# Five instead of four pairs of token chunks through the seven-product form of an output projection

## The chip, the core and the metric

The kernel runs on one core of one Trainium2 chip. The metric is the device time of one execution in microseconds (us); lower is better. The engines are named as the profile names them: PE (TensorE, matmul), PEld (its weight load), DVE (VectorE), ACT (ScalarE), POOL (GpSimd) and SP (SyncE). SP issues almost all transfers here, and its queue is worked off in order: a transfer that must wait holds everything behind it.

## What is computed

One encoder layer over 2048 tokens of width 1024. A combined input projection feeds a gated linear attention (four heads) and a latent attention (four heads, swept in query blocks). Their outputs are joined to a row of width 1024, multiplied by one 1024x1024 matrix, added to the scaled input, and normalised:

```python
return jnp.concatenate([o_a, o_b], axis=-1) @ w_out
...
x = layer_norm(DEEPNORM_ALPHA * x + mixed, ln_g[layer], ln_b[layer])
```

Only the last two steps, the output projection with its residual and LayerNorm, are touched by the change.

## The kernel before

The tokens are cut into 16 chunks of 128. Every matmul in full precision is done as three matmuls on a high and a low part of each operand (`mm3`: high by high, high by low, low by high), so each left operand is first split: ACT copies it to the rounded high part (`hi`), POOL subtracts to get the low part (`lo`).

The output projection starts while the last attention block is still running and then fills the rest of the program. For chunk c, `load` fetches the attention outputs `oa` (group A) and `ob` (group B) into a tile `of`, and two factors (`gm`, the gate, and `r`, the softmax's reciprocal) into `gr`; `gate` multiplies `ob` by both on POOL; `load_res` fetches the input rows `xr`. A plain chunk is 8 steps of the inner dimension k by two halves n of 512 columns, three matmuls each: 48 matmuls of 128x512 into two PSUM banks. `residual` then adds the scaled input on DVE and takes statistics, `finish_a` and `finish_b` normalise (two DVE instructions each per chunk), and two stores of 256 KB go out. `banks` says which PSUM banks a chunk uses: `pS` (two tiles of two banks) or the single banks `mb`, `x`, `o`, `ap`.

Chunks 8 to 15 go in four pairs through `Pair`. A pair is a 2x2 block product: two row blocks (the two chunks) by two halves of the inner dimension, against a 2x2 cut of the matrix. It is done in seven products of half the inner dimension instead of eight (P1 to P7, 12 matmuls each, 84 for a pair where two plain chunks have 96). For that, sums of the left blocks are formed on DVE (`add`: S1 to S4), seven operands are split instead of four per two chunks, and the products are added up on DVE (`sum`, `read`) with two copies by ACT (`copy`). The sums of weight blocks lie in DRAM as `wt1` to `wt4` and are fetched by `fetch_t`; `wt4` replaces, in place, the second column half of the first four rows of the matrix, which plain chunks need, so it is fetched after the last plain chunk has used them. In a pair P1 writes bank `mb` (`pw0`), P5 bank `x` (`pw1`), P6 bank `o` (`pw2`) and P3 bank `ap` (`pw3`).

Two more pieces of work belong to this stretch. The last attention block (number 15) is closed late: `tot`, `oh`, `ol` prepare its sum and split its output, `tsum` and `turn` are transposes, `y` a product of three matmuls into bank `o`, and `yc` and `rows` are ACT copies that are stored. And `ln_psum` copies the LayerNorm scale and shift from SBUF into a PSUM tile, after which their SBUF tiles `lng` and `lnb` serve odd pairs as `of` tiles.

The order of instructions is given by hand: `PLACE_PAIR` holds, for each step of a pair, its time relative to the pair's start, `PAIR_US` the distance of two pairs, and `put` collects steps that are then sorted by place. Inside `fixed()` ACT, POOL and SP keep the order in which the code is written. `PAIR0` is the first chunk of the first pair.

Of the kernel before, what the change touches and what calls it, by code (L numbers as in the profile page):

```python
# [9 lines left out]
F32 = mybir.dt.float32  # L10
# [8 lines left out]
P = 128  # L19
# [3 lines left out]
NCH = S // P  # L23
# [4 lines left out]
QB = 512  # L28
# [102 lines left out]
)  # L131


PAIR0, PAIR_US = 8, 19.05
PLACE_PAIR = dict(
    load3=(-29.4, -31.5),
    load2=(-25.5, -31.5),
# [252 lines left out]
class K:  # L390
# [1224 lines left out]
    def attention(self):  # L1615
# [4 lines left out]
        with ExitStack() as ctx:  # L1620
# [147 lines left out]
            def tsum(i):  # L1768
                d = stt[i]
                d["x"] = close(i, [P, 4, P], f"sx{i}", (pA, "ap"))  # L1770
                for e in range(4 if i == nb - 1 else 2):
                    nc.tensor.transpose(d["x"][:, e], d["as"][:, 0, e * P:(e + 1) * P], self.ident)

            def rcp(i):

                d = stt[i]
                rc = op.sm.tile([P, 4], F32, tag="rc", name=f"rc{i}")
                if i == nb - 1:
                    V.tensor_reduce(rc, d["x"], AX.X, ALU.add)
                else:  # L1780
                    V.tensor_reduce(rc.rearrange("p (e j) -> p j e", e=2),
                                    d["x"][:, 0:2].rearrange("p j (e k) -> p j e k", e=2), AX.X, ALU.add)
                V.reciprocal(rc, rc)
                d["rc"] = rc
# [56 lines left out]
            def put(place, fn, *a):  # L1841
                todo.append((place, len(todo), fn, a))
# [62 lines left out]
            rest = {c: o for c, o in enumerate(first)}  # L1905

            def load(c):
                if c < NCH:
                    rest[c] = dict(c=c)
                    op.load(rest[c])  # L1910

            def split(c):
                if c < NCH:
# [4 lines left out]
                    op.gate(rest[c])  # L1918
                    op.hi(rest[c], 1)
                    op.lo(rest[c], 1)  # L1920

# [2 lines left out]
            with fixed():  # L1924
                load(4)
                for c in (2, 3):
                    op.load_res(rest[c])
                load(5)
                split(4)
                load(6)  # L1930
# [8 lines left out]
                for c in (2, 3):  # L1939
                    op.residual(rest[c], 0)  # L1940
                    op.residual(rest[c], 1)
                    op.finish(rest[c])
            for c in (4, 5):
                with fixed():
                    if c == 4:
                        split(6)
                        pairs[0].load(1)
                        op.product(rest[4])
                    else:
                        op.load_res(rest[6])  # L1950
                        tsum(nb - 1)
                        with self.after(rest[4]["last"]):
                            rcp(nb - 1)
                        op.product(rest[5])
                        op.ln_psum(0)
                        pairs[1].load(0, "of")
                        op.fetch_t("3m")
                        split(7)
                        pairs[0].load(0)
                    op.finish(rest[c])  # L1960
                if c == 4:
                    with self.after(*last.values()), fixed():
                        for f in (tot, oh, ol):
                            f(nb - 1)

            todo.clear()
            half = 5.44
            put(4 * half - 0.01, op.pair_banks)
            for c in (6, 7):
                o, t = rest[c], 2 * half * (c - 6)  # L1970
                if c == 7:
                    put(-1, op.load_res, o)
                for n in range(2):
                    for k in range(NK):
                        put(t + half * n, op.part, o, k, (n,))
                    put(t + half * (2 if c % 2 else n + 1) + 0.05, op.residual, o, n)
                put(t + 2 * half + 1.3, op.finish_a, o)
                put(t + 2 * half + (5 if c == 6 else 4), op.finish_b, o)
            for place, f in ((5.4, turn), (5.41, y), (6.5, rows), (6.51, yc)):
# [10 lines left out]
class Pair:  # L1990
# [131 lines left out]
    def put(self, put, T, last):  # L2122
# [2 lines left out]
        first = P_[("first", "second")[self.p]] if self.p < 2 else {}  # L2125
        if self.p:
            for r in (1, 0):
                at(P_[f"load{self.p}"][r], self.load, r, *(("gr",),) * (self.p == 1 and r == 0))
        for r in range(2):
            at(P_["res"][r], self.load_res, r)  # L2130
# [54 lines left out]
class OutProj:  # L2185
# [140 lines left out]
    def residual(self, o, n):  # L2326
        nc, c = self.nc, o["c"]
        if n == 0:
            o["rr"] = self.bp.tile([P, 2, 512], F32, tag="ph", name=f"rr{c}", bufs=3)
            o["bn"] = self.sm.tile([P, 2, 6], F32, tag="bn", name=f"bn{c}")  # L2330
        rr = o["rr"][:, n]
        nc.vector.scalar_tensor_tensor(rr, o["xr"][:, n], ALPHA, o["ps"][n], ALU.mult, ALU.add)
        o["last"] = nc.vector.bn_stats(o["bn"][:, n], rr).ins
# [103 lines left out]
```

## Time and profile before

| what | us |
|---|---|
| time, median of 3 runs | 1276.11 (1275.75 to 1276.61) |
| the profiled execution's own time | 1276.71 |
| its span in the trace | 1274.9 |
| first plain matmul of chunk 4 | 1145.86 |
| first product of the first pair | 1190.67 |
| last matmul starts | 1266.86 |

Times inside the trace count from the span's start. A row of the timeline gives start, duration, engine, line, operation, output and input tiles, how many instructions were merged (x2), and in brackets how long the engine sat idle just before and what ended it.

### The profile page before, as it was taken

The numbers are of one execution on the slowest core, as the hardware profiler recorded it, in microseconds if no ns is written. First come the engines' busy times: TensorE is split into PE (matmuls) and PEld (weight loads), VectorE is DVE, ScalarE is ACT, GpSimd is POOL, SyncE is SP. The second block draws the span as 40 slices with busy tenths as digits, with TensorE's granted clock in tenths as the row PEclk, the third lists the DMA queues.
The fourth block names the chain that finished last, engine by engine and source line by source line (L and its number), as shares of the span: only waits on it lengthen the run. The fifth ranks groups of instructions, "written<-read, shape, count | busy, mean of one in ns | idle before, by whom it ended". The sixth has DMA issues, their size and how long they took to land.

```text
span 1274.9 us, 20185 instructions
## 1 busy us (share of the span) xinstructions
PE 1254.0 (98%) x6928; PEld 1109.7 (87%) x6928; DVE 939.2 (74%) x1704; ACT 873.7 (69%) x1537; POOL 849.5 (67%) x550
## 2 busy tenths in 40 slices
PE   7999999999999999999999999999999999999997
PEld 7999999999999999999788888888888888788886
DVE  6866675656675455555798888888888889738887
ACT  7765656766676656665588888888888888624355
POOL 0144545363667666672188888889999999965774
PEclk9999999999999999999999999999999999999999
DMA  9332524343675565555501111122223111568962
GB/s 300 98 94 63 170 79 159 102 156 102 196 249 172 179 220 183 182 198 170 170 1 42 42 43 42 42 58 59 59 58 91 52 43 31 173 207 295 355 200 100
DMA packets 122662, 166.81 MB, mean 131 GB/s; under 512 B 18518, under 2 KB 71390, under 8 KB 121920
## 3 DMA queue, kind: packets, MB, share of 16 engines
q1 hardware_dynamic: 114400, 163.39, 40.1%
q0 software_dynamic: 768, 2.10, 0.5%
q8 instruction: 55, 0.90, 0.3%
q10 hardware_dynamic: 7392, 0.03, 0.3%
q14 instruction: 47, 0.39, 0.1%
HBM read 106.72 MB, written 58.75 MB: 130 GB/s over the span
## 4 chain that ended last, share of the span: by engine, by line
PE 65%; ACT 2%; DVE 1%; POOL 1%; issue 1%; DMA 0%; DVEq 0%; ACTq 0%
PE pS L1649 4%; PE o L456 4%; PE o L454 4%; PE o L455 4%; PE pS L1650 4%; PE pS L1651 4%; PE pS L1652 4%; PE pS L1653 4%; PE pz L455 2%; PE pz L456 2%; PE pz L454 2%; PE pw L455 2%; PE pw L454 2%; PE pw L456 2%; PE ipm L456 1%; PE ipm L454 1%
## 5 line engine op out<-in xcount | busy, mean ns | idle before, releaser
L406 POOL TENSOR_TENSOR pl<-s,ph 128x1024 fp32r<-128x1024 f32 x128 | 306.1, 2415 | 56.5 <-ACT ph L400 56.5
L1671 DVE TENSOR_TENSOR rm<-pS,rm 128x512 f32<-128x512 f32 x210 | 144.7, 689 | 26.4 <-ACT s L1658 20.8
L1695 DVE TENSOR_TENSOR s<-s,mb 128x1024 f32<-128x1024 f32 x128 | 151.2, 1213 | 9.4 <-PE mb L1689 9.3
L1658 ACT ACTIVATE s<-pS 128x1024 f32<-128x1024 f32 x128 | 131.4, 1026 | 37.7 <-PE pS L1653 33.5
L400 ACT ACTIVATE ph<-s 128x1024 fp32r<-128x1024 f32 x128 | 135.0, 1057 | 13.4 <-PE o L456 12.7
L1699 ACT ACTIVATE s<-s 128x1024 f32<-128x1024 f32 x128 | 131.5, 1051 | 13.4 <-DVE s L1695 13.3
L454 PE MATMUL ipa<-wah,xah 128*128 128x384 f32 (+1 forms) x384 | 130.2, 339 | 6.7 <-ACT wah L400 6.7
L1112 POOL TENSOR_TENSOR Us<-Us,cw 128x512 f32<-128x512 f32 x16 | 18.2, 1135 | 175.4 <-DVE Us L1110 167.4
L456 PE MATMUL ipa<-wah,xal 128*128 128x384 f32 (+1 forms) x384 | 125.3, 326 | 0.0
L455 PE MATMUL ipa<-wal,xah 128*128 128x384 f32 (+1 forms) x384 | 125.0, 325 | 0.0
L1649 PE MATMUL pS<-qh,ckvT_h 128*128 128x512 f32 x256 | 102.6, 401 | 0.8 <-DVE rm L1671 0.4
L454 PE MATMUL o<-ph,vh 128*128 128x512 f32 x256 | 101.1, 395 | 0.0
L1650 PE MATMUL pS<-ql,ckvT_h 128*128 128x512 f32 x256 | 99.9, 390 | 0.0
L1651 PE MATMUL pS<-qh,ckvT_l 128*128 128x512 f32 x256 | 99.9, 390 | 0.0
L1652 PE MATMUL pS<-rh,krs 128*128 128x512 f32 x256 | 99.8, 390 | 0.0
L1653 PE MATMUL pS<-rl,krs 128*128 128x512 f32 x256 | 99.8, 390 | 0.0
L456 PE MATMUL o<-ph,vl 128*128 128x512 f32 x256 | 99.8, 390 | 0.0
L455 PE MATMUL o<-pl,vh 128*128 128x512 f32 x256 | 99.7, 389 | 0.0
L1722 DVE TENSOR_TENSOR ap<-ap,s 128x512 f32<-128x512 f32 x120 | 83.0, 692 | 3.5 <-ACT s L1699 0.9
L454 PEld LDWEIGHTS ipa<-wah,xah 128*128 128x128 f32 x384 | 73.4, 191 | 7.3 <-ACT wah L400 6.7
L454 PE MATMUL pz<-xch,wzh 128*128 128x256 f32 x256 | 74.8, 292 | 0.0
L455 PEld LDWEIGHTS ipa<-wal,xah 128*128 128x128 f32 x384 | 73.5, 191 | 0.8 <-DVE wal L406 0.2
(447 smaller groups left out, 3895.4 us busy)
## 6 DMA issues: line engine op xcount, KB each, us to landing
xcf<-xT_dram SPq DMA_DIRECT2D x16, 512.0 KB, 5.0
xr<-x_dram SPq DMA_DIRECT2D x16, 512.0 KB, 6.4
xaf<-xT_dram SPq DMA_DIRECT2D x14, 512.0 KB, 3.8
wb<-wO_dram SPq DMA_DIRECT2D x16, 256.0 KB, 3.0
oib<-oi_s SPq DMA_DIRECT2D x16, 256.0 KB, 4.3
qdb<-qd_s SPq DMA_DIRECT2D x16, 256.0 KB, 4.5
SU<-su_s SPq DMA_DIRECT2D x16, 256.0 KB, 4.7
ub<-u_s SPq DMA_DIRECT2D x16, 256.0 KB, 4.3
```

The costliest lines, as they stand in the source:

```text
L400: return nc.scalar.activation(dst, src, AF.Copy).ins
L406: return e.tensor_tensor(dst, src, hi.bitcast(F32), ALU.subtract).ins
L454: mm(out, ah, bh, start=start, stop=False)
L455: mm(out, ah, bl, start=False, stop=False)
L456: mm(out, al, bh, start=False, stop=stop)
L1649: mm(ps[:, e], kh, qh, start=True, stop=False)
L1650: mm(ps[:, e], kh, ql, start=False, stop=False)
L1651: mm(ps[:, e], kl, qh, start=False, stop=False)
L1652: mm(ps[:, e], kr, rh, start=False, stop=False)
L1653: mm(ps[:, e], kr, rl, start=False, stop=True)
L1671: V.tensor_tensor(d["rm"], src[:, e], d["rm"], ALU.max)
L1695: V.tensor_tensor(s, s, d["mb"][:, None, :].to_broadcast([P, 2, QB]), ALU.subtract)
```

## The change

`PAIR0` goes from 8 to 6: chunks 6 and 7 become a pair, and only chunks 0 to 5 are plain. Everything else adapts the surroundings. Chunks 4 and 5 both use the single banks `mb` and `x` (before, chunk 5 had a `pS` tile). Chunk 5 adds its residual in the tile of its input rows. `yc` gets the buffer `ofh` in place of `ofl`, which the first pair's copies use. The written order of the stretch ahead of the pairs changes: loads, splits, `finish` calls and the closing of block 15 are interleaved differently, and in `PLACE_PAIR` the first pair's residual loads and one gate move. The first pair now loads where the plain chunk 6 did.

```diff
-PAIR0, PAIR_US = 8, 19.05
+PAIR0, PAIR_US = 6, 19.05
...
-    gate0=((-6.0, -4.7), (-24.72, -21.3)),
+    gate0=((-11.0, -10.9), (-24.72, -21.3)),
...
-    first=dict(hA11=-15.2, hS3=-8.0, hA12=0.9, lS3=-6.5, aS4=0.3, hS4=0.35, lS4=0.4),
+    first=dict(res=(-18.7, -18.6), hA11=-15.2, hS3=-8.0, hA12=0.9, lS3=-6.5, aS4=0.3, hS4=0.35, lS4=0.4),
...
-                t = bp.tile([P, QB], F32, tag="ofl", name=f"yc{i}", bufs=1)
+                t = bp.tile([P, QB], F32, tag="ofh" if i == nb - 1 else "ofl", name=f"yc{i}", bufs=1)
...
+                op.finish(rest[0])
+                split(4, 0)
+                op.finish(rest[1])
+                split(4, 1)
+                op.residual(rest[2], 0)
+                op.residual(rest[2], 1)
+                pairs[0].load(1)
                 op.load_res(rest[4])
-                for c in (0, 1):
-                    op.finish(rest[c])
-                split(5)
-                load(7)
+                with self.after(*last.values()):
+                    for f in (tot, oh, ol):
+                        f(nb - 1)
+                split(5, 0)
+                op.finish(rest[2])
+                split(5, 1)
+                pairs[0].load(0)
                 op.load_res(rest[5])
                 op.fetch_t("2l")
                 op.fetch_t("3h")
...
-            for c in (6, 7):
-                o, t = rest[c], 2 * half * (c - 6)
-                if c == 7:
-                    put(-1, op.load_res, o)
+            for c in (4, 5):
+                o, t = rest[c], 2 * half * (c - 4)
...
-            put(17.15, op.fetch_t, "4h")
-            put(17.16, op.fetch_t, "4l")
+            put(1.5, op.ln_psum, 0)
+            put(5.6, op.finish_a, rest[3])
+            put(10.96, op.finish_b, rest[3])
+            put(6.4, pairs[1].load, 0, "of")
+            put(11.9, op.fetch_t, "3m")
+            put(17.05, op.fetch_t, "4h")
+            put(17.06, op.fetch_t, "4l")
...
-        if c == PAIR0 - 1:
-            return [p.tile([P, 512], F32, tag=t, name=f"p{t}{c}") for p, t in self.single[2:]]
-        if c < 2 or c % 2:
+        if c < 2 or c == PAIR0 - 3:
             ps = self.ps.tile([P, 2, 512], F32, tag="pS", name=f"po{c}")
...
-            o["rr"] = self.bp.tile([P, 2, 512], F32, tag="ph", name=f"rr{c}", bufs=3)
+            o["rr"] = o["xr"] if c == PAIR0 - 1 else self.bp.tile([P, 2, 512], F32, tag="ph", name=f"rr{c}", bufs=3)
```

The first place is DVE where chunk 1 is finished and chunk 2's two banks (`pmb2`, `px2`) are read, which chunk 4's matmuls write next. `rr` is a chunk's result tile, the number behind a name its chunk. Before:

```order
L1743 COPY acc15_12969<-ap15_12370 128x512
L2345 BN_AGGR mv1_12785<-bn1_12678 128x2
L2346 TENSOR_SCALAR u1_12786<-mv1_12785 128x1
L2348 SCALAR_TENSOR_TENSOR rr1_12677<-rr1_12677,mv1_12785,lng_12573 128x512 x2
L2332 SCALAR_TENSOR_TENSOR rr2_12826<-xr2_12738,pmb2_12557 128x512
```

The same place on DVE now, from the second half of chunk 1's residual on:

```order
L2352 SCALAR_TENSOR_TENSOR rr0_12647<-rr0_12647,ln0_r_12758,lnb_12574 128x512
L2318 BN_STATS bn1_12678<-rr1_12677 128x6
L1743 COPY acc15_12811<-ap15_12370 128x512
L2330 BN_AGGR mv1_12774<-bn1_12678 128x2
L2331 TENSOR_SCALAR u1_12775<-mv1_12774 128x1
L2333 SCALAR_TENSOR_TENSOR rr1_12677<-rr1_12677,mv1_12774,lng_12573 128x512 x2
L2352 SCALAR_TENSOR_TENSOR rr1_12677<-rr1_12677,ln1_r_12784,lnb_12574 128x512 x2
L2317 SCALAR_TENSOR_TENSOR rr2_12798<-xr2_12738,pmb2_12557 128x512
```

The two closing instructions of chunk 0 and the two of chunk 1 now stand ahead of the read of `pmb2`; before, all four stood behind it.

The second place is SP behind chunk 5's loads. Before:

```order
L2277 DMA of5_12742<-ob_s1_165 128x4x128
L2274 DMA of6_12758<-oa_s6_150 128x512
L2275 DMA gr4_12733<-gm_s1_141 128x4x128
L2276 DMA gr4_12733<-r_s1_161 128x4x128
L2277 DMA of6_12758<-ob_s1_165 128x4x128
L2296 DMA xr4_12763<-x_dram 128x1024
L2368 DMA out_dram<-rr0_12647 128x512 x2
L2368 DMA out_dram<-rr1_12677 128x512 x2
```

And now:

```order
L2264 DMA of5_12742<-ob_s1_165 128x4x128
L2353 DMA out_dram<-rr0_12647 128x512 x2
L2353 DMA out_dram<-rr1_12677 128x512 x2
L2000 DMA of6_12804<-oa_s6_150 128x512
L2003 DMA gr4_12733<-gm_s1_141 128x4x128
L2004 DMA gr4_12733<-r_s1_161 128x4x128
L2006 DMA of6_12804<-ob_s1_165 128x4x128
L2283 DMA xr4_12809<-x_dram 128x1024
L2353 DMA out_dram<-rr2_12798 128x512 x2
```

The four stores of chunks 0 and 1 moved from behind chunk 4's input rows to ahead of chunk 6's loads.

The third place is DVE from chunk 4's closing to the first pair's first read. `pw0` is the bank that chunk 5 calls `pmb5`. Now:

```order
L2027 TENSOR_TENSOR of7_12849<-s1_0_12996,of7_12849 128x512
L2352 SCALAR_TENSOR_TENSOR rr4_12928<-rr4_12928,ln4_r_13013,ln1_12821 128x512 x2
L2317 SCALAR_TENSOR_TENSOR xr5_12854<-xr5_12854,pmb5_12961 128x512
L2318 BN_STATS bn5_13058<-xr5_12854 128x6
L2317 SCALAR_TENSOR_TENSOR xr5_12854<-xr5_12854,px5_12962 128x512
L2318 BN_STATS bn5_13058<-xr5_12854 128x6
```

Before, the last plain chunk (7) stood there with the banks `o` and `ap`, which the first pair needs only at its third and fourth product:

```order
L2367 SCALAR_TENSOR_TENSOR rr6_13147<-rr6_13147,ln6_r_13206,ln1_13050 128x512 x2
L2332 SCALAR_TENSOR_TENSOR rr7_13284<-xr7_13084,po7_13161 128x512
L2333 BN_STATS bn7_13285<-rr7_13284 128x6
L2332 SCALAR_TENSOR_TENSOR rr7_13284<-xr7_13084,pap7_13162 128x512
L2333 BN_STATS bn7_13285<-rr7_13284 128x6
```

Chunk 5's first bank is now the one that the pair's first product writes.

More of the change, by code (lines that the diff above doesn't have):

```diff
@@ L1907, in load, with split @@
             def load(c):
[L1908 to L1913, printed above, removed]
+                rest[c] = dict(c=c)
+                op.load(rest[c])
+            def split(c, j):
+                if j == 0:
                     op.hi(rest[c], 0)
@@ L1918, in split @@
                     op.gate(rest[c])
+                else:
                     op.hi(rest[c], 1)
@@ L1938, in attention @@
                 op.fetch_t("3h")
[L1939 to L1964, printed above, removed]
+                op.residual(rest[3], 0)
+                op.residual(rest[3], 1)
             todo.clear()
@@ L1975, in attention @@
                         put(t + half * n, op.part, o, k, (n,))
-                    put(t + half * (2 if c % 2 else n + 1) + 0.05, op.residual, o, n)
+                    put(t + half * (n + 1) + 0.05, op.residual, o, n)
                 put(t + 2 * half + 1.3, op.finish_a, o)
-                put(t + 2 * half + (5 if c == 6 else 4), op.finish_b, o)
-            for place, f in ((5.4, turn), (5.41, y), (6.5, rows), (6.51, yc)):
+                put(t + 2 * half + (5 if c == 4 else 4), op.finish_b, o)
+            for place, f in ((10.87, tsum), (10.9, rcp), (21.7, turn), (21.71, y), (22.0, rows), (22.01, yc)):
                 put(place, f, nb - 1)
-            put(17.15, op.fetch_t, "4h")
-            put(17.16, op.fetch_t, "4l")
+            put(1.5, op.ln_psum, 0)
[5 more added lines that the diff above has]
+            put(17.06, op.fetch_t, "4l")
             for q in pairs:
@@ L2127, in put @@
             for r in (1, 0):
-                at(P_[f"load{self.p}"][r], self.load, r, *(("gr",),) * (self.p == 1 and r == 0))
+                at(P_[f"load{min(self.p, 3)}"][r], self.load, r, *(("gr",),) * (self.p == 1 and r == 0))
         for r in range(2):
-            at(P_["res"][r], self.load_res, r)
+            at(first.get("res", P_["res"])[r], self.load_res, r)
             for n in range(2):
```

2 lines of the change are left out of this document (removed).

## The prediction

> **What bounds the kernel now.** I read the busy shares first, then what PE waited for in the last 215 us, then the stretches around the change, and last the timelines of the engines that hand PE its operands and banks.
>
> ```profile
> span 1274.9 us, 20185 instructions
> PE 1254.0 (98%) x6928; PEld 1109.7 (87%) x6928; DVE 939.2 (74%) x1704; ACT 873.7 (69%) x1537; POOL 849.5 (67%) x550
> ```
>
> The busy shares alone only say that PE has the least slack. The waits of PE from 1060 us to the end decide:
>
> ```profile
> PE y L454 <- DVE rc L1781: 0.3, 1, 0.3
> ```
>
> That row (waiter, releaser, us in total, times, longest) is the whole answer: one wait of 0.3 us, at block 15's `y`. So PE sets the end from there on, and a matmul taken away in this stretch is time taken away, as long as nothing makes PE wait. How long a matmul is, and which places I follow, comes from PE's timeline (start, duration):
>
> ```profile
> 1145.86 0.39 PE L454 MATMUL pmb<-woh,oh 128*128 128x512 f32 x1
> 1151.30 0.39 PE L454 MATMUL px<-woh,oh 128*128 128x512 f32 x1
> 1157.11 0.48 PE L454 MATMUL po<-woh,oh 128*128 128x512 f32 x1
> 1190.67 0.39 PE L454 MATMUL pw<-woh,A11h 128*128 128x512 f32 x1
> 1209.26 0.39 PE L455 MATMUL pw<-wol,A22h 128*128 128x512 f32 x1
> ```
>
> Between the first matmul of chunk 4's first half and that of its second lie 24 matmuls: 5.44 us, 0.2267 us each (the 0.39 is one matmul's own length, which overlaps the next). The third row is chunk 5's first matmul, the fourth the first product of the first pair, the fifth the last low piece of `wt4`, in P4.
>
> **What the change takes away.** Chunks 6 and 7 cost 2 x 48 = 96 matmuls as plain chunks and 7 x 12 = 84 as a pair; the order of PE has 6582 rows for 6594. 12 x 0.2267 = **2.72 us** off PE, of which all is on the path. Without a new wait chunks 4 and 5 stay where they are, and everything from the first pair on comes 96 x 0.2267 = 21.76 us earlier, with one more pair behind it: P1 at 1168.9, the last low piece of `wt4` needed at 1187.5. P5 follows P1 at once, and so on every 2.72 us.
>
> **What it adds.** DVE gets 10 rows more (sums of blocks and products), POOL 4 (splits), ACT 11, SP none. Ten at 0.69 us are 6.9 us for DVE, four at 1.29 us are 5.2 us for POOL. These lie beside PE, which has a whole chunk or pair to cover them:
>
> ```profile
> 1140.00:1150.00 10.00, 10.00 (x46) 8.29 (x45) 5.03 (x9) 3.69 (x12) 4.28 (x4) 1.00 0.77 251
> 1150.00:1160.00 10.00, 10.00 (x48) 8.30 (x47) 8.42 (x12) 1.91 (x6) 5.55 (x4) 1.00 0.83 278
> 1180.00:1190.00 10.00, 10.00 (x46) 8.26 (x45) 8.89 (x14) 4.10 (x10) 4.68 (x4) 1.00 1.10 361
> 1200.00:1210.00 10.00, 10.00 (x46) 8.29 (x45) 7.40 (x12) 3.42 (x6) 8.57 (x8) 1.00 1.04 367
> 1147.60:1206.00 58.40, 58.40 (x262) 48.25 (x261) 49.55 (x78) 21.20 (x57) 36.84 (x28) 1.00 0.95 324
> ```
>
> The columns are stretch, length, then busy time (and count) of PE, PEld, DVE, ACT and POOL, the granted PE clock, the DMA share and GB/s. Inside a pair (1200 to 1210) DVE has 2.6 us free of 10 and POOL 1.4, with PE gapless; one more such pair costs nothing of itself. If that cover were gone, the added work would cost up to DVE's 6.9 us. So the question is only the join: chunks 4 and 5 and the first pair, where DVE is at 8.4 and 8.9 of 10. There are five places where something now stands closer to PE than before.
>
> **Place 1, chunk 4's first bank.** Chunk 4 writes `pmb` at 1145.86 only when chunk 2's residual has read it. Before, that read stood ahead of the closing instructions (`finish_b`) of chunks 0 and 1; now it stands behind all four of them.
>
> ```profile
> 1136.43 0.69 DVE L2332 SCALAR_TENSOR_TENSOR rr<-xr,po 128x512 f32<-128x512 f32 x1 [0.47 <-DMA xr<-x_dram]
> ...
> 1139.97 1.41 DVE L2348 SCALAR_TENSOR_TENSOR rr<-rr,mv,lng 128x512 f32<-128x512 f32 x2
> 1144.23 0.69 DVE L2332 SCALAR_TENSOR_TENSOR rr<-xr,pmb 128x512 f32<-128x512 f32 x1 [2.86 <-POOL of L2283]
> ...
> 1147.64 3.85 DVE L2367 SCALAR_TENSOR_TENSOR rr<-rr,ln_r,lnb 128x512 f32<-128x512 f32 x4 [2.12 <-ACT ln_r L2359]
> ...
> 1153.03 2.19 DVE L2348 SCALAR_TENSOR_TENSOR rr<-rr,mv,lng 128x512 f32<-128x512 f32 x2
> 1156.12 1.47 DVE L2367 SCALAR_TENSOR_TENSOR rr<-rr,ln_r,lnb 128x512 f32<-128x512 f32 x2 [0.89 <-ACT ln_r L2359]
> ...
> 1163.30 2.45 DVE L2367 SCALAR_TENSOR_TENSOR rr<-rr,ln_r,lnb 128x512 f32<-128x512 f32 x2
> ...
> 1175.18 1.39 DVE L2348 SCALAR_TENSOR_TENSOR rr<-rr,mv,ln 128x512 f32<-128x512 f32 x2
> ...
> 1186.55 1.51 DVE L2040 TENSOR_TENSOR of<-s,of 128x512 f32<-128x512 f32 x1
> ```
>
> I walk DVE from 1136.43, which the landing of chunk 1's input rows sets. Before, `finish_a` of chunk 1 ends at 1139.97 + 1.41 = 1141.38. Now chunk 0's two closing pieces stand ahead of it: a pair of them takes 1.47 when undisturbed and up to 2.45, so it ends at 1142.8 to 1143.8. Chunk 1's two pieces follow, again 1.47 to 2.45, hence 1144.3 to 1146.3 at the ends; then the residual, 0.69, hands over the bank at 1145.0 to 1146.9, against 1145.86. Both pairs at their worst is not to be had, since POOL is idle under the first (below), so I take 1144.9 to 1146.4 as bounds: a wait of 0 to 0.5, and I take 0.1, because the row nearest to it (1147.64, four pieces with POOL at work beside some of them, 1.9 a pair) gives 1145.9.
>
> ```profile
> 1142.87 2.67 POOL L2283 TENSOR_TENSOR of<-of,gr 128x512 f32<-128x512 f32 x2 [3.86 <-DMA of<-ob_s]
> ...
> 1150.90 3.12 POOL L2283 TENSOR_TENSOR of<-of,gr 128x512 f32<-128x512 f32 x2
> ```
>
> These two rows are POOL's gates of chunks 4 and 5. Beside the second, DVE's two pieces at 1153.03 took 2.19 where the same form with its scale in PSUM took 1.39 at 1175.18, and the gate itself took 3.12 for 2.67: each is slowed by 0.45 to 0.8 us. The first gate will now stand beside chunk 1's closing pieces.
> The Trainium skill, SBUF — State Buffer, Who interferes with whom, says that a VectorE instruction with two SBUF inputs contends with a GpSimd instruction that reads SBUF, through a shared pair of ports that is an exclusive lock. By that rule each of the two closing pieces could wait for a whole gate instruction, and the sum would be some 1.6 us worse (an estimate from this page); the rows above agree with it in the direction but show half of the size.
>
> **Place 2, chunk 5's first bank.** It is now `mb`, the one that chunk 4 has just left, at 1157.11; before, it was a free tile. Chunk 4's residual needs its input rows:
>
> ```profile
> 1139.97 2.61 SPq L2277 DMA_DIRECT2D of<-ob_s  x1
> 1147.60 0.32 SPq L2274 DMA_DIRECT2D of<-oa_s  x1
> ...
> 1149.83 0.56 SPq L2296 DMA_DIRECT2D xr<-x_dram  x1
> ...
> 1194.47 2.12 SPq L2243 DMA_DIRECT2D woh<-wt4h_s  x4
> 1196.69 3.29 SPq L2243 DMA_DIRECT2D wol<-wt4l_s  x4
> 1200.52 0.98 SPq L2368 DMA_DIRECT2D out_dram<-rr  x2
> ...
> 1205.34 0.73 SPq L2024 DMA_DIRECT2D xr<-x_dram  x1
> ```
>
> ```profile
> xr<-x_dram SPq DMA_DIRECT2D x12, 512.0 KB, 6.4
> out_dram<-rr SPq DMA_DIRECT2D x16, 256.0 KB, 6.9
> ...
> wol<-wt4l_s SPq DMA_DIRECT2D x4, 256.0 KB, 6.7
> ...
> DMA to landing us min/median/max: 3.6/6.6/9.5
> ```
>
> These are SP's issues (start, length), and then the kilobytes and median landing times of the transfers from 1120 on, with the spread of landing for `xr` up to 1170. The rows for chunk 4 are issued at 1149.83, right behind the loads that wait until 1147.60 for their tile. The four stores now ahead of these loads fall into SP's gap from 1142.58 to 1147.60: chunk 0's can go from 1143 on, chunk 1's at the latest from 1146.3, and at some 0.5 us an issue (1200.52) SP is through by 1147.3. At the median the rows land at 1156.2, at the fastest at 1153.4; the residual of 0.69 ends by 1157.0, against 1157.11. At 9.5 it would be 1159.3 + 0.7, a wait of 2.9. I take 0, from the median.
>
> **Place 3, P1's bank.** Chunk 5's residual must read `pmb5` before P1 writes it at 1168.9. On DVE between chunk 4's first read and that stand chunk 4's other read, two `finish_a`, two `finish_b`, the reduction of block 15 and three sums of the new pair: 18 pieces of 512 columns and small ones, at 0.69 each 12.0 us; with the disturbed sizes (2.45 for one `finish_b`, or 1.51 for a sum at 1186.55) 13.3. From a start at 1155.0 to 1156.8 it ends at 1167.0 to 1170.1: a wait of 0 to 1.2. The middle, 1168.5, is 0.4 ahead of PE; I take 0.
>
> **Place 4, `wt4`.** It overwrites matrix rows that chunk 5 reads to its end, and must be in place at 1187.5. Before, it was issued at 1194.47 to 1199.98 and landed by 1206.7, with 2.6 us to spare to 1209.26. Now the queue has to carry, from 1147.60 up to its end, 46 pieces of 256 KB (before: 69), counted from SP's order: 12.06 MB. At the 324 GB/s of the stretch 1147.60 to 1206.00 that is 37.2 us, done at 1184.8: 2.7 us to spare. I take 0; the bound is under rival C.
>
> **Place 5, the second pair's input rows.** Before, the second pair's rows (chunk 11) were issued at 1205.34, 4.4 us ahead of the second pair (1190.67 + 19.05). Now four more issues stand between `wt4` and the rows of chunk 9 (two factors, block 15's two outputs), which by the pace of the rows above (0.5 to 1 us each) brings them 2 to 4 us closer to the pair that uses them, almost to its start. They are needed only where its first sum of products reads them, and landing at 6.4 leaves DVE waiting some 2 us of the 2.6 in 10 that it has free. I take 0, bound 1.
>
> ACT's 11 rows find 8 us free of 10 (1150 to 1160). The tail, from the last pair on, is the same code.
>
> **The sum.** -2.72 + 0.1 = -2.6 us. The profiled execution took 1276.71 (span 1274.9 and 1.8 around it), so a profile of the changed kernel should show 1274.1; it stands 0.6 above the median of the runs, so against 1276.11 the forecast is **1273.5**.
>
> **The rivals.** That the change doesn't do what it says is excluded: PE's order has the 12 rows less, at 0.2267 each.
> A: DVE hands over a bank late (places 1 to 3). For it: 8.42 and 8.89 of 10 busy, and margins of 0.4 us or less against disturbances of 0.8. Against: the rows' middle values just fit. A wait of 0.3 to 1.7; typical 1.0, giving 1274.4. The exclusive lock is this case at its worst: the two pieces at 1143 to 1146 behind a gate instruction of 1.3 us, 1.6 in all, giving 1275.1.
> B: SP's queue is late, with `wt4` or the second pair's rows (places 4 and 5): the issues are in order, and `woh` and `wol` took 5.5 us to issue. A wait of 0.3 to 5, typical 2, giving 1275.5.
> C, on the other side: the transfers are slower, since the same queue now has stores, loads and `wt3` in 40 us. The row 1140 to 1150 shows 251 GB/s, and at that rate 12.06 MB take 48.0 us, to 1195.6: P4 waits 8.1, giving 1281.5. It decides from 5.3 us of wait on (2.72 and 2.55 more), that is `wt4` at 1192.8, or below 12.06 / 45.2 = 0.267 MB per us. Against it: that row stands where SP was idle for 5 us; 1180 to 1190 and 1200 to 1210, with a full queue, show 361 and 367.
>
> **How the numbers follow.** No wait of more than 0.2 us: 0.46. A: 0.25, of which the lock 0.08. B: 0.12. C: 0.17, which also holds the 9.5 us landing at place 2 together with a late place 3. The prediction is that of the first, 1273.5. The bound of 0.2% (about what a measurement of this kernel can tell from no change) is 2.55 us, so faster means below 1273.56: the forecast lies only just there, and faster gets 0.46. A and B end within 0.2%: 0.37. Slower: 0.17. The range runs from 1273.0 (all covers hold, and the runs' own 0.4 below their median) to 1276.6, which takes in A whole and B but for its end; this leaves out about 2 in 10.
>
> **What the profile after would show.** Right: PE's products 2.72 us apart from 1168.9 on, P4's last low piece at 1187.5, no row of PE's waits above 0.3, and a span of about 1272.3. Place 1 wrong: PE waits at `pmb` at 1145.9 for DVE `rr`. Place 2: the same at 1157.1, with DVE waiting for `xr`. Place 3: PE waits at `pw` at 1168.9 for DVE `xr`. Place 4 or C: PE waits at `pw` around 1185 for a transfer of `woh` or `wol`, with GB/s under 270 in the 40 us ahead of it. Place 5: PE waits at a product of the second pair, with DVE waiting for `xr`. If DVE's disturbed pieces (2.2 to 2.5 us a pair) show up in the rows and PE still does not wait, the margins were larger than my walk has them.

## The result and the profile after

The changed kernel takes **1277.9 us** (median of 22 runs, 1275.35 to 1281.27) against 1276.11 us for the kernel before (22 runs on the same chips, 1275.26 to 1277.84): a ratio of 1.0014, with a 95% interval of 1.0007 to 1.0020. It is slower by 1.8 us, which is within the 0.2% named in the prediction but clear of the noise, and it lies above the predicted range (1273.0 to 1276.6). The profiled execution took 1277.54 us.

The 12 matmuls are gone, and PE has the same work per matmul. What PE waited for from 1060 us to the end, however, is now a list (waiter, releaser, us in total, times, longest):

```profile
span 1275.8 us, 20183 instructions
...
PE 1251.9 (98%) x6916; PEld 1105.9 (87%) x6916; DVE 943.9 (74%) x1710; ACT 880.0 (69%) x1551; POOL 853.0 (67%) x553
```

```profile
PE pw L454 <- ACT pc L2052: 1.9, 3, 1.1
PE pmb L454 <- DVE rr L2317: 0.8, 2, 0.6
PE y L454 <- DVE rc L1781: 0.3, 1, 0.3
PE pw L454 <- DVE xr L2317: 0.3, 1, 0.3
```

PE was busy 2.1 us less than before (1254.0), most of the 2.72 us, but it waits 3.0 us where it waited for nothing: at chunk 4's and chunk 5's first bank (`pmb`, 0.6 and 0.2), at the first pair's P1 (`xr`, 0.3), and, for most of it, at P1 of the third, fourth and fifth pair, each time for `pc`, ACT's copy of the bank that P7 wrote in the pair before. PE's own timeline gives the places:

```profile
1145.36 0.47 PE L454 MATMUL pmb<-woh,oh 128*128 128x512 f32 x1 [0.60 <-DVE rr L2317]
...
1157.13 0.47 PE L454 MATMUL pmb<-woh,oh 128*128 128x512 f32 x1 [0.20 <-DVE rr L2317]
...
1169.34 0.47 PE L454 MATMUL pw<-woh,A11h 128*128 128x512 f32 x1 [0.26 <-DVE xr L2317]
...
1207.93 0.50 PE L454 MATMUL pw<-woh,A11h 128*128 128x512 f32 x1 [0.23 <-ACT pc L2052]
...
1228.42 0.50 PE L454 MATMUL pw<-woh,A11h 128*128 128x512 f32 x1 [1.07 <-ACT pc L2052]
...
1248.45 0.50 PE L454 MATMUL pw<-woh,A11h 128*128 128x512 f32 x1 [0.60 <-ACT pc L2052]
```

Since chunk 4 is reached a microsecond or more earlier or later in different executions (1144.6 here, 1145.86 before), I compare two stretches and not the ends. The **join** runs from the moment chunk 4 could have started (the start of the matmul before it, plus 0.2267) to P1 of the first pair; the **pairs** run from there to the start of the last matmul. Before, the join took 44.81 us and the four pairs 76.19, which is 19.05 a pair, without a wait. Less two plain chunks (21.76) the join should take 23.05 now, and five pairs 95.24. It took 24.74 and the pairs 98.36: **1.69 us lost at the join and 3.12 in the pairs**, 4.8 in all against 2.72 saved, so 2.1 us more.

How the pairs come to wait can be followed in the third and fourth pair (P1 at 1207.93 and 1228.42). SP issues the third pair's input rows, DVE waits for them, and ACT takes up the next pair's operands and the copy:

```profile
1187.20 1.35 SPq L2011 DMA_DIRECT2D xr<-x_dram  x2
...
1208.14 1.41 SPq L2011 DMA_DIRECT2D xr<-x_dram  x2
...
1227.62 1.37 SPq L2011 DMA_DIRECT2D xr<-x_dram  x2
```

```profile
1194.77 0.69 DVE L2062 SCALAR_TENSOR_TENSOR xr<-xr,pw 128x512 f32<-128x512 f32 x1 [1.03 <-DMA xr<-x_dram]
...
1215.25 0.69 DVE L2062 SCALAR_TENSOR_TENSOR xr<-xr,pw 128x512 f32<-128x512 f32 x1 [1.44 <-DMA xr<-x_dram]
...
1235.28 0.69 DVE L2062 SCALAR_TENSOR_TENSOR xr<-xr,pw 128x512 f32<-128x512 f32 x1 [1.45 <-DMA xr<-x_dram]
```

```profile
1226.73 0.63 ACT L400 ACTIVATE S2h<-lng 128x512 fp32r<-128x512 f32 x1 [2.02 <-DVE lng L2027]
1227.27 0.61 ACT L400 ACTIVATE S3h<-lnb 128x512 fp32r<-128x512 f32 x1
1227.79 0.58 ACT L2052 ACTIVATE pc<-pw 128x512 f32<-128x512 f32 x1
```

The rows were asked for at 1208.14 and DVE could use them at 1215.25, 7.3 us after its pair's start. The sums S2 and S3 for the next pair stand behind that on DVE, ACT waits 2.02 us for S2, and the copy `pc` stands behind S2h and S3h in ACT's order, although P7 had filled its bank by about 1221.7. From DVE's read of the late rows to the end of `pc` it is 13.1 us (1215.25 to 1228.37), so a pair keeps its distance only if that read comes no later than about 5.9 us after its P1 (19.05 - 13.1). In the changed kernel it came at 6.3, 7.3 and 6.9. The other pairs bear this out: after the reads at 6.3 (second pair, P1 at 1188.50) and 6.9 the next P1 came 0.4 and 1.0 us later than 19.05. In the kernel before, the third pair's rows were issued, and the reads of the second and third pair stood, here (their P1 first):

```profile
1225.88 1.32 SPq L2024 DMA_DIRECT2D xr<-x_dram  x2
```

```profile
1209.71 0.39 PE L454 MATMUL pw<-woh,A11h 128*128 128x512 f32 x1
...
1228.75 0.39 PE L454 MATMUL pw<-woh,A11h 128*128 128x512 f32 x1
```

```profile
1213.63 0.67 DVE L2075 SCALAR_TENSOR_TENSOR xr<-xr,pw 128x512 f32<-128x512 f32 x1
...
1233.95 0.69 DVE L2075 SCALAR_TENSOR_TENSOR xr<-xr,pw 128x512 f32<-128x512 f32 x1 [0.95 <-DMA xr<-x_dram]
```

With P1 at 1209.71 and 1228.75 these are 3.9 and 5.2 us: it was inside the limit, but the rows had already slipped from 4.4 us ahead of the second pair to 2.9 ahead of the third. (The last pair's rows, which have only stores ahead of them on SP, were issued 5.9 us ahead; the change adds one more pair of the other kind.)

### The profile page after: what moved, and what is told of

Its sections match the earlier page's. It is cut to its first block, busy times and chain, and to the rows that moved or that the text cites. A ratio compares the mean times of both kernels' runs of the same rounds, so it can differ in the third digit from the quotient of the medians.

```text
span 1275.8 us, 20183 instructions
## 1 busy us (share of the span) xinstructions
PE 1251.9 (98%) x6916; PEld 1105.9 (87%) x6916; DVE 943.9 (74%) x1710; ACT 880.0 (69%) x1551; POOL 853.0 (67%) x553
## 4 chain that ended last, share of the span: by engine, by line
PE 78%; DVE 6%; DMA 6%; ACT 3%; POOL 3%; issue 2%; SPq 1%; DVEq 0%; POOLq 0%; ACTq 0%
PE pS L1649 4%; PE pS L1651 4%; PE pS L1650 4%; PE pS L1653 4%; PE pS L1652 4%; PE o L454 4%; PE o L455 4%; PE o L456 4%; PE ipa L454 4%; PE ipa L456 4%; PE ipa L455 4%; PE pz L455 2%; PE pz L456 2%; PE pz L454 2%; PE ipg L454 2%
```

## The experiments

My theory (L) was that late input rows make DVE late, and that ACT's order turns this into a wait of PE. The rivals were J, that the lateness comes from the join and only runs on, and for the rows' lateness S, that the transfers are saturated, against Q, that the queue's order sets it. In this table the losses at the join and in the pairs are worked out from PE's records as above, from one profiled execution each; the time is the median of 10 or 11 runs (22 for the first two; the kernel before took 1276.2 to 1276.7 beside the others). Five of the kernels leave the join as the change made it (changed, rows earlier, copy earlier, both, `wt4` an eighth), and they lost 1.39 to 2.50 there, so a difference of a microsecond at the join between two profiles shows nothing by itself.

| kernel | lost at the join | lost in the pairs | time |
|---|---|---|---|
| before | 0 | 0 | 1276.1 |
| changed | 1.69 | 3.12 | 1277.9 |
| rows earlier | 1.82 | 3.00 | 1277.5 |
| copy earlier | 2.01 | 1.53 | 1276.6 |
| rows and copy earlier | 2.50 | 0.12 | 1275.7 |
| before, one pair's rows late | 0.01 | 1.56 | 1277.7 |
| before, rows and copy earlier | 0.00 | 0.00 | 1276.3 |
| `wt4` an eighth | 1.39 | 2.11 | 1276.8 |
| bank first | 7.02 | 0.02 | 1279.5 |
| no gate of chunk 4 | 0.54 | 2.79 | 1277.3 |
| own tile, bank first, copy earlier | 4.29 | 0.60 | 1278.4 |
| join's rows, rows and copy earlier | 0.99 | 1.01 | 1274.8 |
| the same, bank first | 1.14 | 0.12 | 1275.5 |
| the same, P1's bank first | 0.52 | 1.39 | 1274.8 |

### The rows earlier

```diff
-    res=(-10.0, -8.0),
+    res=(-15.5, -15.4),
```

> The input rows of pairs 2 to 5 are issued ahead of the stores and tile loads that stood before them on SP (place -15.5 for -10). Theory L (late rows: SP issues the rows about when the pair starts, DVE's first sum waits for them 1.0 to 1.5 us, DVE is late with S2 and S3, ACT's in-order queue holds the copy pc behind S3h, and the next P1 waits for pc): DVE no longer waits for xr, PE's waits for pc (1.9 us in three places) fall to under 0.3, the time comes 2 to 3 us below the changed kernel's 1277.9: 1275 to 1276. Rival J (the lateness comes from the join, chunks 4 and 5, and only runs on through DVE): the waits for pc stay at 1 to 2 us, time 1277 to 1278. Rival D (transfers are slower now): rows still land 7 us after their issue, but early, so as L; the loads behind them come later and PE waits for an operand instead.

1277.49 us, ratio to the kernel before 1.0002 (0.9993 to 1.0011). DVE waited for no pair's rows any more, and still PE lost as much in the pairs, now at one place:

```profile
PE pw L454 <- ACT pc L2052: 2.5, 1, 2.5
```

```profile
POOL lng L2015 <- DMA gr<-gm_s: 2.8, 1, 2.8
POOL of L2015 <- DMA of<-ob_s: 2.6, 1, 2.6
```

```profile
1209.98 0.63 ACT L400 ACTIVATE S2h<-of 128x512 fp32r<-128x512 f32 x1 [4.02 <-DVE of L2027]
1210.52 0.61 ACT L400 ACTIVATE S3h<-of 128x512 fp32r<-128x512 f32 x1
1211.04 0.58 ACT L2052 ACTIVATE pc<-pw 128x512 f32<-128x512 f32 x1
```

The loads that the rows had overtaken were late instead: POOL waited for gate factors and for rows of `ob`, ACT waited 4.02 us for the third pair's S2, and `pc` stood behind it again. Late rows are thus not the only way into the wait; any late operand leads there, because of where `pc` stands. Theory L in the form that I had put down, rows alone, missed with its 1275 to 1276.

### The copy earlier

```diff
-    ... c7=14.91, ...
+    ... c7=11.9, ...
```

> On ACT the copy of P7's bank (pc) stands ahead of the next pair's S2h and S3h instead of behind them; the rows stay where they are. L: the rows are as late as before (DVE waits some 1.4 us for xr), but PE's waits for pc are gone (0), since the copy needs only P7's end at 13.6 us and the bank is free 5 us ahead of the next P1; DVE no longer sits idle 1.8 us a pair for pc. Time 1275 to 1275.6. J: the same if only ACT's order matters, with DVE still late. If the copy is not what holds P1, PE's waits move to another row (P5 or P3 for an operand) and the time stays at 1277 to 1278.

1276.59 us, ratio 1.0001 (0.9992 to 1.0010), above the 1275 to 1275.6 expected. PE has no wait for `pc` left, and DVE's 1.8 us of idling for it in each pair are gone. DVE now waits for the rows up to 4.4 us, and the next thing in line shows:

```profile
PE pw L454 <- DVE xr L2062: 1.1, 1, 1.1
```

```profile
DVE xr L2062 <- DMA xr<-x_dram: 6.9, 3, 4.4
```

P2 waits once for its bank, which a sum reads that itself waited for rows. The loss in the pairs is halved: half of it was ACT's order, half the rows themselves.

### Rows and copy

The two edits above together.

> The pairs' input rows earlier on SP and the copy pc ahead of S2h. Alone, the first moved the lateness to the loads behind it (POOL waited 2.6 and 2.8 us for gate factors and rows of ob, ACT held pc behind A12h, P1 of the third pair waited 2.5 us), the second left P2 waiting 1.1 us for a sum that waited for rows. Together: no row is late for DVE and no copy stands behind a late operand; PE waits only at chunks 4 and 5 (1.5 us in the two profiles): 1275 to 1275.8. If S holds in full, the late operand of the third pair itself (A12) shows as a wait at P2 of over 1 us: 1276.5.

1275.68 us, ratio 0.9998 (0.9990 to 1.0007). In the pairs PE waits for nothing, and 0.12 us are lost there; what remains is the join (beside block 15's 0.3):

```profile
PE pmb L454 <- DVE rr L2317: 1.5, 2, 0.9
PE pw L454 <- DVE xr L2317: 0.3, 1, 0.3
```

So the pairs' loss is explained by these two causes, and J is out: the join was no better here (2.50 lost), and the pairs lost nothing.

### The kernel before, with one pair's rows late

```diff
-            at(P_["res"][r], self.load_res, r)
+            at(P_["res"][r] + (4.0 if self.p == 1 else 0.0), self.load_res, r)
```

> The kernel before, with only the second pair's input rows moved on SP behind the loads of chunk 13 (issued some 4 to 5 us later, about when that pair starts). L: DVE waits 2 to 3 us for xr in the second pair, the third pair's P1 waits 1 to 2 us for pc, and since the stores behind that DVE work hold the next rows on SP, the third and fourth pairs' rows come late too: time 1277.5 to 1279 for 1276.1. J or D: late rows alone cost nothing (DVE has 2.6 us of 10 free), the time stays at 1276.1 within 0.4.

1277.69 us, ratio 1.0013 (1.0005 to 1.0022). This is the counterproof: the join of this kernel loses nothing, and one pair's rows issued five microseconds later on SP (1210.45 for 1205.34) cost it 1.2 us.

```profile
PE pw L454 <- ACT pc L2065: 0.9, 1, 0.9
```

```profile
1216.44 0.69 DVE L2075 SCALAR_TENSOR_TENSOR xr<-xr,pw 128x512 f32<-128x512 f32 x1 [2.81 <-DMA xr<-x_dram]
...
1235.72 0.69 DVE L2075 SCALAR_TENSOR_TENSOR xr<-xr,pw 128x512 f32<-128x512 f32 x1 [0.55 <-DMA xr<-x_dram]
```

The read came 7.0 us after its P1 (1209.46) and the next P1 waited 0.9, as the limit of 5.9 says. The next pair's rows were late too (1229.44 on SP, 0.2 ahead of P1 where it had been 2.9), but with 6.1 us that read was only just over the limit. The chain of lateness from pair to pair exists and dies out here, which I had expected to be stronger.

### The kernel before, with both edits

The edits of the first two experiments, in the kernel before.

> The kernel before with the same two edits (rows of all pairs earlier, pc ahead of S2h). PE waited for nothing there, so by every theory on the pairs the time stays within 0.4 us of the kernel before (1276.1); if it falls by 1 us or more, the two edits gain something that has nothing to do with the fifth pair, and their gain in the changed kernel must be read against that.

1276.27 us, ratio 0.9998 (0.9989 to 1.0008). They gain nothing there, so what they gain in the changed kernel is what its pairs had lost.

### `wt4` at an eighth of its bytes

```diff
-                sync.dma_start(self.W[k][p][:, 512:].bitcast(F32), kern.wt_s[j][p][:, k])
+                sync.dma_start(self.W[k][p][:, 512:576].bitcast(F32), kern.wt_s[j][p][:, k, :64])
```

> The eight transfers of wt4 move an eighth of their bytes (64 of 512 columns; P4's other weights stay those of the plain matrix, so P4 is computed with wrong weights). 1.84 MB less, 5.6 us at 330 GB/s, with as many issues. Theory S (the transfers are saturated from 1142 to 1195 us, DMA share 1.0, and what stands behind wt4 comes late for that reason): the second pair's rows land 4 to 6 us earlier, DVE waits for none of them in that pair, PE's waits for pc vanish, time 1274.5 to 1275.7. Theory Q (the order of the queue, not its bytes): the rows still wait behind the same issues, the waits for pc stay at over 1 us, 1277 to 1278.

1276.80 us, ratio 1.0003 (0.9994 to 1.0012): neither theory's number. The transfers were less busy in the stretch from `wt4`'s last issue to the rows (the columns are as in the prediction; DMA share and GB/s stand last), first in the changed kernel, then here:

```profile
1180.00:1187.20 7.20, 7.20 (x34) 5.95 (x33) 4.83 (x7) 2.53 (x5) 4.53 (x4) 1.00 1.03 350
```

```profile
1178.80:1185.80 7.00, 7.00 (x33) 5.79 (x32) 4.64 (x7) 2.79 (x5) 5.02 (x5) 1.00 0.83 213
```

```profile
1175.91 2.87 SPq L2230 DMA_DIRECT2D wol<-wt4l_s  x4
...
1185.80 1.09 SPq L2011 DMA_DIRECT2D xr<-x_dram  x2
```

SP still needed 7.0 us from there to the rows, against 7.3 (1179.87 to 1187.20), and issued them 1.5 us ahead of the second pair, against 1.3. The DMA share fell from 1.03 to 0.83 and the rows were as late, so for the second pair the order and pace of SP's queue set the time of issue (Q), not the bytes. The later pairs have no `wt4` near their rows, and the run says nothing of them. The second pair's read nevertheless came 0.5 us earlier after P1 (5.7), the third pair's P1 did not wait, and the fourth's and fifth's still waited 0.7 and 0.5. How much of the 7 us from issue to use is queueing I did not separate.

### Chunk 2's banks read first

```diff
-                op.finish(rest[1])
+                op.finish_a(rest[1])
                 split(4, 1)
                 op.residual(rest[2], 0)
                 op.residual(rest[2], 1)
+                op.finish_b(rest[1])
```

> Chunk 1's closing pieces stand behind the reads of chunk 2's banks on DVE again (chunk 0's stay ahead). All agree that PE's wait at chunk 4's first bank (0.6 us) goes. J: the pairs start 0.6 us earlier, their waits fall too, time 1276.5 to 1277. L: the pairs' rows are set by SP, whose chain does not start at PE: the waits for pc grow by up to 0.6, time 1277.3 to 1278.

1279.52 us, ratio 1.0024 (1.0015 to 1.0033): slower, against all theories. The wait at chunk 4 went, and a larger one came at chunk 5:

```profile
PE pmb L454 <- DVE rr L2318: 4.1, 1, 4.1
```

```profile
1159.77:1165.03 5.26, 5.26 (x13) 4.10 (x13) 5.16 (x11) 1.90 (x6) 2.43 (x2) 0.50 1.03 381
```

The second row (columns as in the prediction) shows the matmuls behind that wait: 13 of them ran at a granted clock of 0.50, and the 24 of this half took 8.21 us for 5.44. So 4.1 us of waiting and 2.8 of slow matmuls make up most of the 7.02 lost at the join. What held DVE is this:

```profile
1158.94 0.69 DVE L2318 SCALAR_TENSOR_TENSOR rr<-xr,pmb 128x512 f32<-128x512 f32 x1 [4.01 <-DMA out_dram<-rr]
```

Chunk 4's result goes into a buffer that an earlier chunk's store must leave. The expectations below take this for chunk 1's, but chunk 1's two stores had landed by 1150.0 here (1149.1 in the changed kernel). The semaphores that the residual waits for are those of its own input rows and of chunk 2's two stores, and the trace has the rows landed at 1157.44 and the stores at 1158.74. Chunk 1's closing pieces had held up its stores on SP (the four issues of chunks 0 and 1 took 7.49 us for 4.43), and behind these came the rows and chunk 2's stores. In the changed kernel the same wait is there, 1.75 us on DVE, of which 0.20 reach PE; the rows landed at 1154.57, chunk 2's stores, whose issue is the first row here, at 1156.11:

```profile
1151.52 1.00 SPq L2353 DMA_DIRECT2D out_dram<-rr  x2
```

```profile
1156.30 0.69 DVE L2317 SCALAR_TENSOR_TENSOR rr<-xr,pmb 128x512 f32<-128x512 f32 x1 [1.75 <-DMA out_dram<-rr]
```

The changed kernel's order of closing steps keeps that wait short. The pairs lost nothing in this run: starting some 5 us later against the same queue (P1 at 1174.23 for 1169.34) they had their rows in time, which is again theory L and speaks against J.

### Chunk 4 without its gate

```diff
-                    op.gate(rest[c])
+                    if c != 4:
+                        op.gate(rest[c])
```

> POOL's two gate instructions of chunk 4 are left out (so chunk 4's group B rows are not gated; nothing else changes). If POOL's gate is what slows chunk 1's closing pieces on DVE (3.32 us for two beside it, against 1.40 undisturbed), they take 1.4 to 1.5 us and PE's wait of 0.6 us at chunk 4's first bank is gone; if something else slows them, 3.3 stays. The pairs' rows still come late, so the time falls by at most 0.6 (J) or not at all, the waits for pc growing instead (L): 1277 to 1278.

1277.25 us, ratio 1.0005 (0.9996 to 1.0014). The wait at chunk 4 is gone. Chunk 1's two closing pieces took 3.32 us in the changed kernel and 2.45 here, which lies between the two values expected:

```profile
1141.30 3.32 DVE L2352 SCALAR_TENSOR_TENSOR rr<-rr,ln_r,lnb 128x512 f32<-128x512 f32 x2
```

```profile
1142.50 2.45 DVE L2353 SCALAR_TENSOR_TENSOR rr<-rr,ln_r,lnb 128x512 f32<-128x512 f32 x2
```

POOL's work beside them was the gate, and here one split:

```profile
1140.90 3.16 POOL L2270 TENSOR_TENSOR of<-of,gr 128x512 f32<-128x512 f32 x2 [3.08 <-DMA of<-ob_s]
```

```profile
1143.06 1.33 POOL L406 TENSOR_TENSOR ol<-of,oh 128x512 fp32r<-128x512 f32 x1 [4.04 <-ACT oh L400]
```

Undisturbed the two pieces take 1.40 to 1.47. Beside two POOL instructions they take 3.32, 1.9 more; beside one, 2.45, 1.0 more: in these rows each POOL instruction costs DVE about 1 us. So the gate is the cause only as the POOL work that happens to be there, and a split does the same. The Trainium skill, SBUF — State Buffer, Who interferes with whom, calls the shared ports an exclusive lock; these rows agree with that roughly for DVE, which loses 1.0 of the 1.3 us of a POOL instruction, while POOL's two lose only 0.5 together.

### Chunk 4 in its own tile

```diff
-            o["rr"] = o["xr"] if c == PAIR0 - 1 else ...
+            o["rr"] = o["xr"] if PAIR0 - 2 <= c < PAIR0 else ...
```

with chunk 2's banks read first and the copy earlier.

> Chunk 1's closing pieces behind the reads of chunk 2's banks, chunk 4's residual in the tile of its own input rows (so that it does not wait for chunk 1's store, which cost 4.0 us when only the closing pieces were moved), and the copy pc ahead of S2h. PE's waits at chunk 4's and chunk 5's first bank go (0.6 and 0.2). The pairs then start about 1 us earlier against the same transfers: by S DVE waits for xr longer, and PE pays at P2 for a part of it (1.1 us with the copy moved alone); by J no wait is left. S: 1275.5 to 1276.5; J: 1273.5 to 1274.5.

1278.36 us, ratio 1.0016 (1.0008 to 1.0025), worse than both theories. The store no longer holds chunk 4's residual, but its input rows do, which stand on SP behind chunk 1's stores and chunk 6's loads:

```profile
PE pmb L454 <- DVE xr L2318: 2.6, 1, 2.6
```

```profile
DVE xr L2318 <- DMA xr<-x_dram: 2.7, 1, 2.7
```

Here too the matmuls behind the wait of 2.6 us ran at a granted clock of 0.50 (seven of them, 1.6 us more), which is part of the 4.29 lost at the join.

### The join's rows, and towards a faster kernel

Three kernels carry the rows and the copy earlier and chunk 4's own tile, and issue chunk 4's input rows right behind chunk 5's loads:

```diff
                 load(5)
+                op.load_res(rest[4])
                 op.finish(rest[0])
...
                 pairs[0].load(1)
-                op.load_res(rest[4])
```

> The rows of the pairs earlier, the copy pc ahead of S2h, and for the join: chunk 4's input rows issued right behind chunk 5's loads, and chunk 4's residual in their tile (so it waits neither for rows nor for chunk 1's store). PE's wait at chunk 5's first bank (0.2 to 0.6) goes, those at chunk 4's first bank (0.6 to 0.9) and at P1 (0.3) stay or shrink, no wait for pc. Against the kernel with the first two edits alone (1275.7): 1275.0 to 1275.5. If the lateness of chunk 4's residual had another cause (DVE itself behind), the wait at chunk 5 stays and the time is 1275.7.

1274.84 us (1273.88 to 1275.44), ratio **0.9987** (0.9978 to 0.9996). The wait at chunk 5 is gone, as expected; that at chunk 4 stayed (0.7), and P6 of the second pair waited 0.7 us, which I had not foreseen: POOL's gate of that pair had waited 3.4 us for its factors, and DVE's sum and read behind it came late.

The second of them also reads chunk 2's banks ahead of chunk 1's closing pieces.

> As the kernel with the join's rows moved, and in addition chunk 1's closing pieces behind the reads of chunk 2's banks on DVE. All of PE's waits at the join go but the 0.3 of block 15; 2.7 us of matmuls saved and nothing given back: 1273.4 to 1274.2. If the stores of chunk 1, now later on SP, hold the loads of chunk 6 behind them, P1 or P5 waits for an operand instead, and the time is 1274.5 to 1276.

1275.53 us, ratio 0.9990 (0.9981 to 0.9999), above the 1273.4 to 1274.2 expected. The waits at chunks 4 and 5 and in the pairs are gone, and one is left:

```profile
PE pw L454 <- DVE xr L2318: 1.0, 1, 1.0
PE y L454 <- DVE rc L1781: 0.3, 1, 0.3
```

It is P1's bank, the third place of the prediction. The third kernel moves chunk 4's last closing step behind the read of that bank.

```diff
-                put(t + 2 * half + (5 if c == 4 else 4), op.finish_b, o)
+                put(t + 2 * half + (5.7 if c == 4 else 4), op.finish_b, o)
```

> As the kernel with all edits at the join, and chunk 4's second closing step behind the first read of chunk 5's bank on DVE (two pieces, 1.40 us, out of the way of P1). The wait of 1.0 us at P1 goes; PE then waits at nothing but block 15's 0.3: the time falls from 1275.5 by 1.0 to 1274.2 to 1274.8, and its profile shows 118.3 to 118.6 us from chunk 4's first matmul to the last one. If the store of chunk 4, now a little later, holds wt4 behind it on SP, P4 waits for a transfer instead and the time stays at 1275.5.

1274.75 us (1273.79 to 1277.12), ratio **0.9985** (0.9976 to 0.9994). P1's wait is gone; in the profiled execution, the slowest of the eleven, P6 of the second pair, chunk 5 and an operand (`S4l`) in the first pair waited 0.5, 0.3 and 0.2 us, so the 118.3 to 118.6 us expected from chunk 4 to the last matmul were 120.2. This kernel and the first of the three are faster than the kernel before by 1.3 to 2.0 us and than the changed one by some 3. The three can't be told apart by their intervals, so that the last edit met its expected time does not show that P1's wait made the difference. Half to three quarters of the 2.72 us is thus to be had.

## Why the prediction was wrong

- **The matmuls removed (2.72 us): right.** The kernel with the least lost in one profile (the join's rows, bank first) needs 119.55 us from chunk 4 to the last matmul, where the kernel before needed 121.01 and none lost would be 118.29. The work added beside PE was less than I had counted: the traces have 6 instructions more on DVE, 3 on POOL and 14 on ACT (busy 4.7, 3.5 and 6.3 us), where the prediction has 10, 4 and 11.
- **"One more such pair costs nothing of itself": the step that failed.** I priced the pairs by busy shares (DVE 2.6 us free of 10). What counts is a date: DVE's read of the rows must come within about 5.9 us of P1. The rows of the kernel before, above, show the reads at 3.9 and 5.2 us; I had looked at PE's waits there, which were none, and not at how much was left.
- **Place 5, the second pair's rows: taken at 0 with a bound of 1, measured 3.12 us in the pairs.** The prediction had the right place (rows issued about when the pair starts) and the right size for DVE's wait (2 us named; 1.0 to 1.45 measured). It did not follow that wait on to ACT, where the copy for the next P1 stands behind operands that DVE makes, and took it for one pair only, though the later pairs' rows stand behind stores that wait for the same DVE. The kernels with rows and copy earlier, and the kernel before with late rows, show both directions.
- **Place 1: taken at 0.1, bound 0.5, measured 0.60 of waiting, with chunk 4's start 0.76 us later than it could have been.** The two closing pieces took 3.32 us; I had capped a pair at 2.45, a row beside which POOL ran one whole instruction and the start of a second (1163.55 and 1165.16), where here it ran two. The estimate of 1.6 us from the Trainium skill's exclusive lock (SBUF — State Buffer, Who interferes with whom) was nearer for the pair of pieces (1.9 more) than my rows, but as a wait of PE it was too high.
- **Place 2: taken at 0, measured 0.20, but for another reason.** Not the input rows held chunk 4's residual; a store did (1.75 us on DVE), by the trace's semaphores that of chunk 2, whose buffer the residual takes over. I had not asked what frees that buffer.
- **Place 3: taken at 0, measured 0.26**, inside its bound of 1.2. Its 18 pieces at 0.69 are 12.4 us and not 12.0; DVE took 12.9, from its start on chunk 4's first bank (1156.30) to the end of its read of `pmb5`.
- **Place 4 and rival C: right.** PE waited for no `wt4`, and the time didn't go there.
- **The rivals.** A and B both happened, at 1.7 and 3.1 us. I had made them alternatives and drawn the range over each alone; their sum, 1276.1 - 2.7 + 4.8 = 1278.2, is near the measured 1277.9 and outside the range. The loss at the join was too short to give the queue time; 5 us more of it did (chunk 2's banks read first).

## What to carry to other kernels

When a stage is repeated once more, look in the old profile at when the late input of each repetition comes, and compare that with the date that it must keep, not with the free share of its engine. An engine that works in order turns one late operand into lateness of everything behind it: a copy that frees a bank for the bottleneck engine belongs ahead of operands that may be late. And small waits at several places can add up when each has its own cause; they are no alternatives by themselves.

## What the runs showed of the hardware

A wait of PE costs more than its length. After the wait of 1.07 us at 1228.42 the next 24 matmuls took 5.66 us, and after that of 0.60 at 1248.45 they took 5.61, against 5.44 without a wait, at a granted clock of 1.00 in each stretch; the first of them is followed after 0.33 us, the next after 0.24, where the steady distance is 0.2267. Over the six waits of the changed kernel this comes to some 0.9 us beside the 3.0 of waiting. Another 1.0 lies in how a wait is counted: from the end of the matmul before, 0.39 us after its start, where the next one would have started after 0.2267. The three come to about the 4.8 lost. Why the matmuls behind a short wait come slower is open.

```profile
1221.74:1227.18 5.44, 5.44 (x25) 4.32 (x23) 4.83 (x8) 1.08 (x2) 1.30 (x1) 1.00 0.76 211
1228.42:1234.08 5.66, 5.66 (x24) 4.53 (x25) 5.27 (x8) 3.19 (x7) 5.66 (x5) 1.00 1.03 337
1248.45:1254.06 5.61, 5.61 (x24) 4.53 (x25) 5.47 (x9) 4.10 (x8) 3.10 (x4) 1.00 0.00 0
```

Longer waits cost the clock. Behind the wait of 4.1 us (chunk 2's banks read first) 13 matmuls, and behind that of 2.57 (chunk 4 in its own tile) seven, came 0.43 us apart at a granted clock of 0.50; behind the wait of 2.50 for `pc` (rows earlier) the clock stayed at 1.00. What decides between the last two no run here shows.
